# Batched 64x64 matrix multiply: two of the eight a tiles loaded by two casting transfers with 8 KB runs

## The chip, the cores and the metric

The kernel runs on one core of one Trainium2 chip. The core has a matrix engine (TensorE), three engines for elementwise work (VectorE, ScalarE, GpSimd), SyncE, which here only issues transfers, and sixteen DMA engines that move data between HBM and the on-chip memory SBUF. The metric is the device time of one execution in microseconds (us). Of the kernel before, three runs gave a median of 133.72 us (133.55 to 133.87).

## What is computed

```python
# a, b: (1024, 64, 64) float32
def reference(a, b):
    return np.matmul(a, b).astype(np.float32)
```

There are 1,024 independent products of 64x64 matrices. 16.8 MB of a and 16.8 MB of b are read, and 16.8 MB are written.

## The kernel before

**Tiles.** The batch is cut into sixteen steps t of 64 matrices (`n_t`), and into eight a tiles s of 128 matrices (`n_s`), so that a tile s serves the steps 2s and 2s + 1. A b tile and an output tile belong to one step, 1 MB each; an a tile is 2 MB in HBM.

**How a is loaded.** `a_v` (L41) cuts an a tile into four quarters h: quarter h holds every fourth matrix, and each of the 128 partitions gets sixteen rows of one matrix, which lie together in HBM: a run of 4 KB. `load_a` (L70) loads quarters 0 to 2 through GpSimd's queue and lets the DMA cast them to bf16 on the way (L74, `a_sb`); quarter 3 goes through SyncE's queue as fp32 (L78, `a_raw`) and is cast by an engine. `a_sb` and `a_raw` each have three buffers (`A_AHEAD`). Tile 0 is loaded apart, all in fp32 and through SyncE and ScalarE (`load_first_a`, L81 to L92).

**How b is loaded and the result stored.** `load_b` (L94) issues even b tiles on SyncE's queue and odd ones on ScalarE's, as fp32 in runs of 512 B; there are three buffers. `cast` (L169) casts a b tile to bf16, on VectorE but for the first and half of the last. Stores (`put`, L194) go through GpSimd's queue up to step 13, and through SyncE's and ScalarE's for steps 14 and 15.

**What is done with a.** The product needs a transposed, and two neighbouring bf16 values are moved as one fp32 element. For tiles 1, 2 and 3 (`ON_DVE`) VectorE transposes in blocks of 32x32: `transpose_dve` (L116) handles two quarters a call, one transpose of 128x512 elements (L128) for a quarter. For quarter 3, ScalarE first casts `a_raw` (L126). The other tiles are regrouped by VectorE (`regroup`, L100; L109 for the cast quarters, L112 for the fp32 one) and transposed by TensorE (`transpose`, L133). `spread` (L146) then copies the transposed a into a block-diagonal matrix, of which there are two (`bd_tiles`); for tiles 1 to 3 these are eight VectorE copies of 32x512 a step (L154), for the others four of 32x1024 (L164).

**What is multiplied.** `multiply` (L187) does four matrix products for each of sixteen groups of four matrices with the block-diagonal a as the weights (L218), and copies the results from PSUM to `o_sb`, mostly on ScalarE (L206).

**Order.** The order of every engine and every queue is that of the program (`tc.manual_schedule()`, L239). Before the loop, the loads of tile 0, of b tiles 0 to 2 and of a tiles 1 and 2 are issued. Step 0 first puts `spread(1)` and `cast(1)` on VectorE, loads b tile 3, multiplies, transposes a tile 1, and then issues the loads of a tiles 3 and 4; tile 4 takes over the buffers of tile 1. Step 1 puts `spread(2)`, `cast(2)` and the load of b tile 4 in front of its product, and both halves of the transposition of a tile 2 behind it; steps 2 and 3 do the halves of tile 3. A store is issued one step after its product.

Of the kernel before, what the change touches and what calls it, by code (L numbers as in the profile page):

```python
# [8 lines left out]
fp32 = mybir.dt.float32  # L9
bf16 = mybir.dt.bfloat16  # L10
# [3 lines left out]
def kernel(  # L14
# [14 lines left out]
    nc = tc.nc  # L29
# [7 lines left out]
    N_BD = 2  # L37
    HOLD = 2
    ON_DVE = (1, 2, 3)

    a_v = a.rearrange("(s g h) (mp v) k -> s h g mp (v k)", h=4, g=32, v=16)  # L41
    b_v = b.rearrange("(t g h) (kp u) n -> t (h kp) g (u n)", h=4, g=16, u=2)
    o_v = out.rearrange("(t gh x) (mo w) n -> t (x mo) gh (w n)", gh=8, x=8, w=4)

    consts = ctx.enter_context(tc.tile_pool(name="consts", bufs=1))
    a_pool = ctx.enter_context(tc.tile_pool(name="a_pool", bufs=A_AHEAD))
    b_pool = ctx.enter_context(tc.tile_pool(name="b_pool", bufs=B_AHEAD))
    work = ctx.enter_context(tc.tile_pool(name="work", bufs=2))
# [13 lines left out]
    a_tiles, b_tiles, abf_tiles, at_tiles, bbf_tiles = {}, {}, {}, {}, {}  # L62
# [5 lines left out]
        return nc.scalar if t == n_t - 1 and lo % 4 == 0 else nc.sync  # L68

    def load_a(s):  # L70

        a_sb = a_pool.tile([128, 3, 16, 64], bf16, name="a_sb")
        for h in range(3):
            nc.gpsimd.dma_start(  # L74
                out=a_sb[:, h, :, :].rearrange("p v k -> p (v k)"), in_=a_v[s, h], single_packet=True
            )
        a_raw = a_pool.tile([128, 16, 64], fp32, name="a_raw")
        nc.sync.dma_start(out=a_raw[:].rearrange("p v k -> p (v k)"), in_=a_v[s, 3])  # L78
        a_tiles[s] = a_sb, a_raw

    def load_first_a():  # L81

# [17 lines left out]
    def regroup(s):  # L100
        a_sb = a_tiles.pop(s)
        a_bf = work.tile([128, 16, 4, 64], bf16, name="a_bf")
        if s == 0:
            for h in range(4):
                copy = nc.scalar.copy if h % 2 else nc.vector.tensor_copy
                copy(a_bf[:, :, h, :], a_sb[h].rearrange("p (v k) -> p v k", v=16))  # L106
        else:
            cast_sb, raw = a_sb
            nc.vector.tensor_copy(  # L109
                a_bf[:, :, 0:3, :], cast_sb[:].rearrange("p h v k -> p v h k")  # L110
            )
            nc.vector.tensor_copy(a_bf[:, :, 3, :], raw[:])  # L112
        abf_tiles[s] = a_bf
        at_tiles[s] = work.tile([128, 32, 4, 4, 4], fp32, name="at_sb")

    def transpose_dve(s, half):  # L116
        cast_sb, raw = a_tiles[s]
        if half == 0:
            at_tiles[s] = work.tile([128, 4, 8, 4, 4, 4], fp32, name="at_sb")
        for h in (2 * half, 2 * half + 1):  # L120
            rows = cast_sb[:, h, :, :] if h < 3 else None
            if h == 3:
                rows = work.tile([128, 16, 4, 64], bf16, name="a_bf")[:, 0:4, :, :].rearrange(
                    "p x y k -> p (x y) k"
                )
                nc.scalar.copy(rows, raw[:])  # L126
            pairs = rows.rearrange("p v k -> p (v k)").bitcast(fp32)
            nc.vector.transpose(  # L128
                at_tiles[s][:, h].rearrange("p g w mp vo -> p w vo g mp"),
                pairs.rearrange("p (vo w kp) -> p w vo kp", vo=4, w=4),  # L130
            )

    def transpose(s, j):  # L133
        a_cols = abf_tiles[s][:].rearrange("p v h k -> p v (h k)").bitcast(fp32)
        for wl in range(2):
            at_ps = t_psum.tile([128, 4, 128], fp32, name="at_ps")
            for vo in range(4):
                nc.tensor.transpose(  # L138
                    at_ps[:, vo, :], a_cols[:, 4 * vo + 2 * j + wl, :], identity[:]
                )  # L140
            nc.scalar.copy(  # L141
                at_tiles[s][:, :, 2 * j + wl, :, :],
                at_ps[:].rearrange("p vo (g mp) -> p g mp vo", mp=4),
            )

    def spread(t):  # L146
        bd = bd_tiles[t % N_BD]
        at_sb = at_tiles[t // 2]
        for h in range(4):
            rows = slice(32 * h, 32 * h + 32)  # L150
            if t // 2 in ON_DVE:
                for i in range(2):
                    block = 32 * (2 * (t % 2) + i)
                    nc.vector.tensor_copy(  # L154
                        bd[rows, 8 * i : 8 * i + 8, :, h, :, :].rearrange(
                            "p g w mp vo -> p (g w) (mp vo)"
                        ),
                        at_sb[block : block + 32, h].rearrange(
                            "p g w mp vo -> p (g w) (mp vo)"
                        ),  # L160
                    )
            else:
                half = slice(16 * (t % 2), 16 * (t % 2) + 16)
                nc.vector.tensor_copy(  # L164
                    bd[rows, :, :, h, :, :].rearrange("p g w mp vo -> p (g w) (mp vo)"),
                    at_sb[rows, half].rearrange("p g w mp vo -> p (g w) (mp vo)"),
                )
# [19 lines left out]
    def multiply(t):  # L187
# [20 lines left out]
        for half in range(2):  # L208
# [19 lines left out]
            if not last:  # L228
                copies = [nc.scalar.copy] * 4
                if half and t % 2 and t > 2 * max(ON_DVE):  # L230
                    copies[2:] = [nc.vector.tensor_copy] * 2
# [7 lines left out]
    with tc.manual_schedule():  # L239
# [7 lines left out]
        make_identity(nc, identity)  # L247
        nc.gpsimd.memset(bd_tiles[1][:, 0:8], 0.0)
        load_a(1)
        load_b(2)  # L250
        nc.gpsimd.memset(bd_tiles[1][:, 8:16], 0.0)
        load_a(2)
        regroup(0)
        transpose(0, 0)
        transpose(0, 1)
        spread(0)
        cast(0)
        for t in range(n_t):
            s, half = t // 2, t % 2
            if t + 1 < n_t:  # L260
                spread(t + 1)
                cast(t + 1)
            if t + B_AHEAD < n_t:
                load_b(t + B_AHEAD)
            if half == 0 and 0 < s < n_s - 1 - A_AHEAD:
                load_a(s + 1 + A_AHEAD)
            if half == 0 and 0 < s < n_s - 1 and s + 1 not in ON_DVE:
                transpose(s + 1, 1)
            multiply(t)
            if t == 0:  # L270
                transpose_dve(1, 0)
                transpose_dve(1, 1)
                a_tiles.pop(1)
                load_a(A_AHEAD)
                load_a(A_AHEAD + 1)
            if t and s + 2 in ON_DVE and (half or s):
                for part in [0, 1] if t == 1 else [half]:
                    transpose_dve(s + 2, part)
                if half:
                    a_tiles.pop(s + 2)  # L280
            elif half == 0 and 0 < s and s + 2 < n_s:
                regroup(s + 2)
            elif half == 1 and s + 2 < n_s:
                transpose(s + 2, 0)
            if t >= HOLD - 1:
                store(t - HOLD + 1)
# [32 lines left out]
```

## Time and profile before

The profiled execution took 133.61 us, of which the span of the program's instructions is 131.8 us.

| What | Value |
|---|---|
| Time of the profiled execution | 133.61 us |
| Span | 131.8 us |
| VectorE busy | 101.8 us (77%) |
| ScalarE busy | 88.1 us (67%) |
| TensorE matmul busy | 59.6 us (45%) |
| GpSimd busy | 31.9 us (24%) |
| Read from HBM and written to it | 33.55 MB and 16.78 MB, 382 GB/s over the span |
| Casting transfers of a (L74) | 21 of 256 KB as landed, 15.9 us from issue to landing in the median |
| Plain transfers of a (L78) | 7 of 512 KB, 17.3 us |
| Stores on GpSimd's queue (L195) | 14 of 1,024 KB, 22.7 us |

In the rows of forty slices each digit is the busy share of one fortieth of the span (3.3 us) in tenths, 9 standing for 90% and more. In the rows of DMA queues, q0 is GpSimd's, q1 SyncE's and q10 ScalarE's; they give packets, megabytes as landed, and the time that the packets took as a share of sixteen engines' span. In the rows by stretch, each engine has its busy time and the number of its instructions, and at the end stand the granted clock of TensorE, the DMA share and GB/s. In a timeline a row gives start, duration, engine (with a q for its queue), line, operation, what is written from what, and how many were merged. In a row of waits stand who waited, for whom, the total in us, how often, and the longest. Beside these views the trace holds a record of every DMA packet, with its start, duration, queue and size as landed.

### The profile page before, as it was taken

Reading aid. Unit: us, or ns where it says so; the run is one execution under the profiler, and the core shown is the slowest. Engines: PE = TensorE matmul, PEld = TensorE weight load, DVE = VectorE, ACT = ScalarE, POOL = GpSimd, SP = SyncE. Lnnn points to the kernel's source line nnn. Section 1 sums busy time; section 2 is a strip of 40 time slices with the busy share of each in tenths; the row PEclk is TensorE's granted clock in tenths of the full one; section 3 lists DMA queues with packets and bytes.
Section 4 is the critical chain, followed back from the end, with each engine's and each line's share of the span. In section 5 each row is a group of like instructions: output and inputs, shape, how many; then the busy total and the mean of one; then the engine's idle time right before and its main releaser. Section 6 shows DMA issues by size and latency. Waiting matters only on the chain.

```text
span 131.8 us, 2750 instructions
## 1 busy us (share of the span) xinstructions
PE 59.6 (45%) x1104; PEld 56.7 (43%) x1104; DVE 101.8 (77%) x144; ACT 88.1 (67%) x158; POOL 31.9 (24%) x43
## 2 busy tenths in 40 slices
PE   0006405730550640908662883299369619465000
PEld 0006305730550630908552872298368618464000
DVE  5930399529999984999999998699999997898300
ACT  2125414999495096492999989469969996549920
POOL 8991000340054000618031204300420302040000
PEclk9999975798568555595999599558968975579855
DMA  3999999999999999999999999999999999999993
GB/s 68 372 334 313 306 313 280 280 311 321 327 299 400 362 306 297 393 393 400 321 285 357 403 395 362 308 299 385 395 391 393 390 390 397 399 395 406 390 383 136
DMA packets 19020, 44.99 MB, mean 341 GB/s; under 512 B 1088, under 2 KB 3136, under 8 KB 19008
## 3 DMA queue, kind: packets, MB, share of 16 engines
q0 software_dynamic: 6832, 20.19, 50.6%
q1 hardware_dynamic: 7120, 14.68, 30.7%
q10 hardware_dynamic: 5056, 9.96, 20.1%
q8 instruction: 8, 0.13, 0.4%
q14 instruction: 4, 0.03, 0.1%
HBM read 33.55 MB, written 16.78 MB: 382 GB/s over the span
## 4 chain that ended last, share of the span: by engine, by line
DMA 53%; ACT 15%; DVE 14%; PE 6%; issue 5%; SPq 2%; ACTq 0%; DVEq 0%
DMA b_sb<-in_b_dram 53%; ACT o_sb L206 12%; PE o_ps L218 6%; DVE at_bd L164 4%; DVE b_bf L173 4%; DVE at_bd L154 2%; ACT b_bf L173 1%; DVE at_sb L128 1%; DVE o_sb L206 1%; DVE a_bf L109 1%; SPq L91 1%; ACT a_bf L126 1%; SPq L97 1%; ACT b_bf L180 1%; DVE a_bf L112 0%
## 5 line engine op out<-in xcount | busy, mean ns | idle before, releaser
L206 ACT COPY o_sb<-o_ps 64x512 f32<-64x512 f32 x112 | 65.0, 581 | 17.9 <-PE o_ps L218 13.5
L218 PEld LDWEIGHTS <-at_bd 128*128 128x128 bf16 x1024 | 45.2, 117 | 52.6 <-DVE b_bf L173 40.5
L218 PE MATMUL o_ps<-b_bf,at_bd 128*128 128x64 bf16 x960 | 45.6, 223 | 48.7 <-DVE b_bf L173 35.0
L164 DVE COPY at_bd<-at_sb 32x1024 f32<-32x1024 f32 x40 | 29.6, 739 | 6.6 <-ACT at_sb L141 5.6
L195 POOL DMA_DIRECT2D out_dram<-o_sb x14 | 15.4, 1103 | 46.1 <-ACT at_sb L141 20.6
L154 DVE COPY at_bd<-at_sb 32x512 f32<-32x512 f32 x48 | 22.0, 457 | 1.1
L74 POOL DMA_DIRECT2D a_sb<-in_a_dram x21 | 12.4, 606 | 38.5 <-DVE at_sb L128 33.2
L173 DVE CAST b_bf<-b_sb 128x2048 bf16<-128x2048 f32 x14 | 17.2, 1227 | 5.2 <-DMA b_sb<-in_b_dram 4.9
L138 PE MATMUL at_ps<-identity,a_bf 128*128 128x128 f32 x80 | 12.9, 329 | 11.0 <-ACT a_bf L106 11.0
L138 PEld LDWEIGHTS at_ps<-identity,a_bf 128*128 128x128 f32 x80 | 11.7, 176 | 11.0 <-issue 11.0
L141 ACT COPY at_sb<-at_ps 128x512 f32<-128x512 f32 x20 | 10.8, 591 | 2.7 <-PE at_ps L138 2.0
L128 DVE STREAM_TRANSPOSE at_sb<-a_sb 128x512 f32<-128x512 f32 x9 | 8.9, 1065 | 0.0
L128 DVE STREAM_TRANSPOSE at_sb<-a_bf 128x512 f32<-128x512 f32 x3 | 3.1, 1049 | 4.0 <-ACT a_bf L126 4.0
L206 DVE COPY o_sb<-o_ps 64x512 f32<-64x512 f32 x8 | 5.5, 690 | 0.2
L106 ACT CAST a_bf<-o_sb 128x1024 bf16<-128x1024 f32 x2 | 2.1, 1045 | 5.0 <-DMA o_sb<-in_a_dram 5.0
L173 ACT CAST b_bf<-b_sb 128x2048 bf16<-128x2048 f32 x1 | 1.9, 1897 | 4.0 <-DMA b_sb<-in_b_dram 4.0
L126 ACT CAST a_bf<-a_raw 128x1024 bf16<-128x1024 f32 x3 | 3.1, 1046 | 1.7 <-DMA a_raw<-in_a_dram 1.7
L109 DVE COPY a_bf<-a_sb 128x3072 bf16<-128x3072 bf16 x4 | 4.2, 1045 | 0.0
L106 DVE CAST a_bf<-o_sb 128x1024 bf16<-128x1024 f32 x2 | 2.8, 1383 | 1.8 <-DMA o_sb<-in_a_dram 1.8
L246 DVE MEMSET at_bd<- 128x4096 f32 x1 | 3.5, 3472 | 0.8 <-issue 0.8
L206 DVE COPY o_sb<-at_ps 64x256 f32<-64x256 f32 x8 | 3.4, 422 | 0.5 <-PE at_ps L218 0.4
L180 ACT CAST b_bf<-b_sb 128x512 bf16<-128x512 f32 x2 | 1.1, 616 | 3.5 <-DMA b_sb<-in_b_dram 3.5
(16 smaller groups left out, 15.4 us busy)
## 6 DMA issues: line engine op xcount, KB each, us to landing
out_dram<-o_sb POOLq DMA_DIRECT2D x14, 1024.0 KB, 22.7
a_sb<-in_a_dram POOLq DMA_DIRECT2D x21, 256.0 KB, 15.9
a_raw<-in_a_dram SPq DMA_DIRECT2D x7, 512.0 KB, 17.3
o_sb<-in_a_dram SPq DMA_DIRECT2D x2, 512.0 KB, 5.9
o_sb<-in_a_dram ACTq DMA_DIRECT2D x2, 512.0 KB, 7.0
out_dram<-o_sb SPq DMA_DIRECT2D x2, 512.0 KB, 5.5
out_dram<-o_sb SPq DMA_DIRECT2D x2, 256.0 KB, 5.2
out_dram<-o_sb ACTq DMA_DIRECT2D x2, 256.0 KB, 4.7
```

What stands on the lines that cost most here:

```text
L74: nc.gpsimd.dma_start(out=a_sb[:, h, :, :].rearrange("p v k -> p (v k)"), in_=a_v[s, h], single_packet=True)
L106: copy(a_bf[:, :, h, :], a_sb[h].rearrange("p (v k) -> p v k", v=16))
L109: nc.vector.tensor_copy(a_bf[:, :, 0:3, :], cast_sb[:].rearrange("p h v k -> p v h k"))
L128: nc.vector.transpose(at_tiles[s][:, h].rearrange("p g w mp vo -> p w vo g mp"), pairs.rearrange("p (vo w kp) -> p w vo kp", vo=4, w=4),)
L138: nc.tensor.transpose(at_ps[:, vo, :], a_cols[:, 4 * vo + 2 * j + wl, :], identity[:])
L141: nc.scalar.copy(at_tiles[s][:, :, 2 * j + wl, :, :], at_ps[:].rearrange("p vo (g mp) -> p g mp vo", mp=4),)
L154: nc.vector.tensor_copy(bd[rows, 8 * i : 8 * i + 8, :, h, :, :].rearrange("p g w mp vo -> p (g w) (mp vo)"), at_sb[block : block + 32, h]. ...
L164: nc.vector.tensor_copy(bd[rows, :, :, h, :, :].rearrange("p g w mp vo -> p (g w) (mp vo)"), at_sb[rows, half].rearrange("p g w mp vo -> p ...
L173: (nc.vector.tensor_copy if t else nc.scalar.copy)(b_bf[:], b_sb[:])
L195: store_queue(t, lo).dma_start(out=o_v[t, :, lo : lo + n, :], in_=o_sb[:, lo : lo + n].rearrange("p gh j wl n -> p (gh j wl n)"),)
L206: copies[2 * par + wl](dst, src)
L218: nc.tensor.matmul(o_ps[:, gl, g % 2, j, :], at_bd[:, j, g, :, u], b_bf[:, g, 64 * u : 64 * u + 64], start=(u == 0), stop=(u == 1),)
```

## The change

The a tiles 2 and 3 (`LONG_RUNS`) are loaded by two casting transfers each instead of three casting ones and a plain one. The view `a_v8` gives a partition 32 rows of one matrix, a run of 8 KB, and a transfer holds every second matrix. Their transposition has one instruction of 128x1024 elements a half, without ScalarE's cast, and `spread` takes its blocks from the new layout. For every tile the cast part and the fp32 quarter now lie in one buffer (`room`) of the same total size.

```diff
+    LONG_RUNS = (2, 3)
+    a_v8 = a.rearrange("(s g h) (mp v) k -> s h g mp (v k)", h=2, g=64, v=32)
...
     def load_a(s):
-        a_sb = a_pool.tile([128, 3, 16, 64], bf16, name="a_sb")
+        room = a_pool.tile([128, 5120], bf16, name="a_sb")
+        if s in LONG_RUNS:
+            a_sb = room[:, 0:4096].rearrange("p (h x) -> p h x", h=2)
+            for h in range(2):
+                nc.gpsimd.dma_start(out=a_sb[:, h, :], in_=a_v8[s, h], single_packet=True)
+            a_tiles[s] = a_sb
+            return
+        a_sb = room[:, 0:3072].rearrange("p (h x) -> p h x", h=3)
         for h in range(3):
-            nc.gpsimd.dma_start(
-                out=a_sb[:, h, :, :].rearrange("p v k -> p (v k)"), in_=a_v[s, h], single_packet=True
-            )
-        a_raw = a_pool.tile([128, 16, 64], fp32, name="a_raw")
-        nc.sync.dma_start(out=a_raw[:].rearrange("p v k -> p (v k)"), in_=a_v[s, 3])
-        a_tiles[s] = a_sb, a_raw
+            nc.gpsimd.dma_start(out=a_sb[:, h, :], in_=a_v[s, h], single_packet=True)
+        raw = room[:, 3072:5120].bitcast(fp32)
+        nc.sync.dma_start(out=raw, in_=a_v[s, 3])
+        a_tiles[s] = (
+            a_sb.rearrange("p h (v k) -> p h v k", v=16),
+            raw.rearrange("p (v k) -> p v k", v=16),
+        )
...
     def transpose_dve(s, half):
+        if s in LONG_RUNS:
+            if half == 0:
+                at_tiles[s] = work.tile([128, 2, 8, 4, 4, 8], fp32, name="at_sb")
+            nc.vector.transpose(
+                at_tiles[s][:, half].rearrange("p g w gm vo -> p w vo g gm"),
+                a_tiles[s][:, half, :].bitcast(fp32).rearrange(
+                    "p (vo w kp) -> p w vo kp", vo=8, w=4
+                ),
+            )
+            return
...
     def spread(t):
...
                     block = 32 * (2 * (t % 2) + i)
+                    src = at_sb[block : block + 32]
+                    if t // 2 in LONG_RUNS:
+                        pair = 2 * (h // 2)
+                        src = src[:, h % 2, :, :, pair : pair + 2, :]
+                    else:
+                        src = src[:, h]
                     nc.vector.tensor_copy(
...
-                        at_sb[block : block + 32, h].rearrange(
-                            "p g w mp vo -> p (g w) (mp vo)"
-                        ),
+                        src.rearrange("p g w mp vo -> p (g w) (mp vo)"),
```

More of the change, by code (lines that the diff above doesn't have):

```diff
@@ L109, in regroup @@
             nc.vector.tensor_copy(
-                a_bf[:, :, 0:3, :], cast_sb[:].rearrange("p h v k -> p v h k")
+                a_bf[:, :, 0:3, :], cast_sb.rearrange("p h v k -> p v h k")
             )
-            nc.vector.tensor_copy(a_bf[:, :, 3, :], raw[:])
+            nc.vector.tensor_copy(a_bf[:, :, 3, :], raw)
         abf_tiles[s] = a_bf
@@ L125, in transpose_dve @@
                 )
-                nc.scalar.copy(rows, raw[:])
+                nc.scalar.copy(rows, raw)
             pairs = rows.rearrange("p v k -> p (v k)").bitcast(fp32)
```

## The prediction

> **What bounds the kernel now.** I read the slices first, then the queues, the stretches, the waits, and last the order of single instructions.
>
> ```profile
> DVE  5930399529999984999999998699999997898300
> ACT  2125414999495096492999989469969996549920
> DMA  3999999999999999999999999999999999999993
> DMA packets 19020, 44.99 MB, mean 341 GB/s; under 512 B 1088, under 2 KB 3136, under 8 KB 19008
> ...
> q0 software_dynamic: 6832, 20.19, 50.6%
> q1 hardware_dynamic: 7120, 14.68, 30.7%
> q10 hardware_dynamic: 5056, 9.96, 20.1%
> ```
>
> The DMA row has a 9 in every slice but the first and the last, and the queues' shares add up to 101.4% of sixteen engines' span. VectorE is the only other row that is near full, and only from slice 9 to slice 34.
>
> ```profile
> core 0: us, PE busy (x) PEld busy (x) DVE busy (x) ACT busy (x) POOL busy (x), PEclk, DMA share, GB/s
> ...
> 20.00:40.00 20.00, 9.35 (x192) 8.87 (x191) 15.75 (x24) 15.95 (x27) 4.87 (x8) 0.70 1.08 305
> ...
> 92.00:117.00 25.00, 15.47 (x301) 14.79 (x302) 23.09 (x30) 18.82 (x35) 5.85 (x5) 0.73 1.03 393
> 117.00:126.00 9.00, 2.38 (x72) 2.14 (x69) 5.39 (x12) 8.48 (x18) 0.07 (x1) 0.88 1.03 397
> 126.00:131.80 5.80, 0.00 (x0) 0.00 (x0) 0.00 (x0) 0.24 (x1) 0.00 (x0) 0.50 0.70 244
> ```
>
> The DMA share is 1.03 to 1.08 in every stretch up to 126 us, the last of them included, where only stores are left. The 305 GB/s of the early stretch is no slack: bytes are counted as they land, and a casting transfer lands half of what it reads. Counted as read, the packet records give 390 to 409 GB/s in every 3 us from 6 to 123 us. So the end is set by the sum of the DMA work, and a wait elsewhere costs time only if it empties the queues. By issues less packets moved, 4 to 7 MB (10 us of work or more) wait in the queues from 10 us to 110 us, 1.4 MB at 122 us. The chain of waits agrees: 53% of it is b tiles in flight.
>
> **The change, part by part.** Durations below are of the profiled execution (133.61 us, span 131.8, 1.8 us around it); the median of the runs is 133.72, and differences carry over to it.
>
> *Packets.* Sorted by queue and size, the packet records have: 4 KB read and cast to 2 KB, 172 ns, 2,688 times; plain packets of 1, 2 and 4 KB, 46, 84 and 159 ns at their undisturbed values, and of 8 KB (ten, loaded with the program) 310 ns at the fastest. Twice 46 less 84 is 8, twice 84 less 159 is 9, twice 159 less 310 is 8: each packet has some 9 ns that do not grow with its bytes. While casts run, packets overlap (share 1.08): from 12 to 15 us one cast and two 2 KB packets, 172 + 95 + 84 = 351 ns by their durations, moved 8 KB of source per engine at 403 GB/s, which is 8192 / 25.2 = 325 ns. So a 4 KB cast really takes 325 - 2 x 84 = 157 ns, as much as a plain one. Tiles 2 and 3 now have 2 x (3 x 128 casts + 128 plain) = 1,024 packets of 4 KB source; they become 2 x 2 x 128 = 512 of 8 KB. No 8 KB cast is in this trace. Lower bound of the saving: the run is moved as two 4 KB pieces, 0. Upper: all of 172 above the 2 x (159 - 84) = 150 ns of data is per packet, 22 ns, which gives 512 x 22 / 16 = 0.70 us. Below zero: 8 KB takes twice 172 with no overlap, 512 x (344 - 2 x 157) / 16 = 0.96 us lost. I take 9 ns, the plain rows' figure, since the cast's true 157 ns is nearest to theirs: 512 x 9 / 16 = 0.29 us saved.
>
> *The plain quarter.* 256 plain packets become cast bytes. Beside casts they took 170 to 172 ns, as a cast does, and 159 alone: 0, within 256 x 13 / 16 = 0.2 us either way.
>
> *Fewer transfers.* Eight transfers become four. Each ends in a 4-byte packet per engine of 9 ns: 4 x 9 = 0.04 us. Nothing else counts, since with queues that never empty one transfer's completion lies under the next one's packets. The Trainium skill's page "DMA: Bandwidth & Descriptors" (Anatomy of one DMA — SWDGE (gpsimd) path) gives each transfer a fixed cost of about 2.0 us besides its bytes; by it alone four fewer would be worth an estimated 8 us, and the DMA row without a gap says that this cost is hidden here.
>
> *Engines.* ScalarE loses two casts of L126 (1.05 us each), and VectorE no longer waits for them; both lie beside the DMA. Eight transposes of 128x512 (L128, 1,065 ns) become four of 128x1024: 8.5 us if time follows elements, 4.3 if it were fixed; I take 8.4. The 32 copies of L154 for tiles 2 and 3 read 16-element blocks that lie 32 apart, where they read on without gaps. They write such blocks already, so I keep 419 ns; the bound is the 690 ns of VectorE's copy of 512 elements at L206, 32 x 0.27 = 8.7 us.
>
> *GpSimd and SyncE queues.* Both parts of a tile now share one buffer. The casts of tile 4 took over only the cast part's buffer of tile 1 (three transposes, 25.2 us); now they wait for ScalarE's cast of tile 1 too, at 28.9. Behind them stands the first store (28.1, then some 30.6). Tile 4 landed at 42.3 and is first read at 59.6, so 17 us cover this. GpSimd's wait at 11.45 (1.67 us, for a free completion slot) goes. On SyncE the plain loads of tiles 2 and 3 go; that of tile 4 waits for the same ScalarE cast as before, with b tile 4 behind it.
>
> ```profile
> 10.05 0.71 SPq L97 DMA_DIRECT2D b_sb<-in_b_dram  x1
> 10.81 18.66 SPq L78 DMA_DIRECT2D a_raw<-in_a_dram  x3
> 29.93 0.82 SPq L97 DMA_DIRECT2D b_sb<-in_b_dram  x1
> ...
> 29.84 3.44 DVE L154 COPY at_bd<-at_sb 32x512 f32<-32x512 f32 x8
> 33.30 1.23 DVE L173 CAST b_bf<-b_sb 128x2048 bf16<-128x2048 f32 x1
> ...
> DVE b_bf L173 <- DMA b_sb<-in_b_dram: 4.9, 3, 2.0
> ```
>
> SyncE issues b tile 2, then three plain quarters back to back, then b tile 4; VectorE casts b tile 2 at 33.30 and waits for b tiles three times in all.
>
> *Whose packets go first.* This is the price of the change. From 12 to 15 us the three queues moved 46, 51 and 53 packets per us: one for one. A queue's share then follows its packet size. Before, of 8 KB per turn 4 KB were b; now, of 12 KB, again 4. Tiles 2 and 3 are 32 such turns of 310 + 2 x 84 = 478 ns, 15 us in which the b queues get 1 MB less. It is the megabyte of plain quarters that SyncE's queue no longer carries, but those stood behind b tile 2. So b tiles 2 and 3 bear it: half a megabyte at 0.1 MB per us (2 KB x 16 per 325 ns) is 5 us. Tile 2 landed at 32.0 and would land at about 37; its cast (33.30, right behind the copies of L154, so just in time) moves to 37.3, and everything on VectorE behind it by 4 us. I put 0 on it, for three reasons. The queues still hold about 2 MB: 6.3 at 42 us, less the plain quarter (0.5), the casts of tile 5 (1.6) and two stores (2.1) that would be issued after that. VectorE later sits idle for b tiles for 2.0 us (until 51.2), 1.6 (83.7) and 1.2 (112.5), 4.8 together (the last line above), and b tile 4 has no plain quarters ahead of it any more. And the last store piece is issued at 126.27 while packets run until 130.6, so some 2 us of lateness stay hidden even at the end. The Trainium skill's "DMA: Bandwidth & Descriptors" (SWDGE vs HWDGE vs iDMA) prefers packets of at most 4096 B, as a DMA engine changes queues only between packets; that rule speaks against 8 KB runs, and its price would be this same delay.
>
> Sum: -0.29 - 0.04 + 0 = -0.33; 133.61 becomes 133.28, the median 133.72 becomes **133.4**.
>
> **Rivals.**
> *The long run is cut* into two 4 KB packets: only 0.04 us is left, 133.7. For it: no dynamic packet here is over 4 KB. Against: plain 8 KB packets exist.
> *A cast of 8 KB stalls its engine* (two times 172, nothing overlapped): 0.96 - 0.04, 134.6. For it: 172 is above the plain 159, and the eight 16 KB packets that load code took 967 ns, over three times the 8 KB ones. Against: the throughput shows the excess hidden.
> *b tile 2 is late and stays late* (the slower side by order, not by work): place, the VectorE cast of b tile 2; it decides once more than 2 us are left at the last tile. If none of the 4 us is made up, 4 - 2 = 2 us, 135.4 with the saving. For it: VectorE is 92% busy from 92 to 117 us. Against: the three idle stretches.
> *The 22 ns are all saved*: 0.70 + 0.04, 133.0.
>
> **How the numbers follow.** Forecast 0.46, cut 0.18, stall 0.15, late 0.14, all saved 0.07. The forecast's own range is 133.2 to 133.6, the 0.2 us either way of the plain quarter. The range 132.9 to 134.7 takes in all but the late b tile, which leaves out some 0.17 in all. About 0.2% (0.27 us) is what a measurement of this kernel can tell from no change. Faster by that: 0.38 of the forecast's 0.46 and the 0.07, 0.45. Same: the rest of the forecast and the cut, 0.26. Slower: 0.29.
>
> **What would show it.** Right: queue 0's packets fall from 6,832 to 6,544 (768 casts become 512, and two transfers of 16 completions go; with the runs cut there are 1,024 casts and it rises to 7,056), 8 KB casts last 310 to 330 ns, DMA stays at 9 throughout, b tile 2 lands near 37 us and VectorE's lateness is gone by its wait near 83 us. Wrong: 8 KB casts of 344 ns, L154's copies of these tiles well over 419 ns, or a slice after 117 us below 9 in the DMA row. That would make the end a matter of order, and my sum of packets would not hold.

## The result and the profile after

The changed kernel took 134.48 us in the median of seven runs (134.06 to 134.92), the kernel before 133.72 us in seven runs on the same chip (133.46 to 133.94): the ratio is 1.0054 (interval 1.0035 to 1.0074). It is slower by 0.7 us, where a gain of 0.33 us was forecast: the interval lies clear of no change, on the other side. The profiled execution took 134.31 us, its span 132.5 us.

The slices, packets and queues of the kernel after:

```profile
DVE  5930197908599999999999999599999998696600
DMA  3999999999999999999999999999999999999993
GB/s 73 360 338 310 307 281 281 249 278 312 301 276 330 400 328 275 361 393 404 323 283 354 399 395 365 306 297 387 398 390 393 388 392 394 398 400 404 391 377 133
DMA packets 18444, 44.47 MB, mean 336 GB/s; under 512 B 1024, under 2 KB 3072, under 8 KB 18432
...
q0 software_dynamic: 6544, 20.71, 51.9%
q1 hardware_dynamic: 6832, 13.63, 28.8%
q10 hardware_dynamic: 5056, 9.96, 20.5%
```

By these lines the change did what it says: queue 0 has 6,544 packets, as worked out, and the DMA row still holds a 9 in every slice but the first and the last. Nothing in that row tells that this execution is slower. The next view is the waits of the kernel after (who waited, for whom, total in us, times, the longest), and after it the timelines of GpSimd, of ScalarE's cast of tile 1 and of VectorE's casts of b, each after and then before:

```profile
POOL a_sb L82 <- ACT a_bf L145: 21.3, 1, 21.3
...
POOL a_sb L82 <- DVE at_sb L129: 18.7, 2, 10.1
```

```profile
30.40 1.74 POOL L82 DMA_DIRECT2D a_sb<-in_a_dram  x3 [21.34 <-ACT a_bf L145]
32.11 0.94 POOL L218 DMA_DIRECT2D out_dram<-o_sb  x1
...
41.63 1.79 POOL L82 DMA_DIRECT2D a_sb<-in_a_dram  x3 [8.59 <-DVE at_sb L129]
```

```profile
25.23 1.61 POOL L74 DMA_DIRECT2D a_sb<-in_a_dram  x3 [13.25 <-DVE at_sb L128]
...
37.65 1.69 POOL L74 DMA_DIRECT2D a_sb<-in_a_dram  x3 [8.62 <-DVE at_sb L128]
```

```profile
29.06 1.05 ACT L145 CAST a_bf<-a_sb 128x1024 bf16<-128x1024 f32 x1
```

```profile
27.85 1.05 ACT L126 CAST a_bf<-a_raw 128x1024 bf16<-128x1024 f32 x1
```

```profile
36.45 1.23 DVE L196 CAST b_bf<-b_sb 128x2048 bf16<-128x2048 f32 x1 [1.40 <-DMA b_sb<-in_b_dram]
...
52.29 1.23 DVE L196 CAST b_bf<-b_sb 128x2048 bf16<-128x2048 f32 x1
...
84.52 1.23 DVE L196 CAST b_bf<-b_sb 128x2048 bf16<-128x2048 f32 x1 [1.56 <-DMA b_sb<-in_b_dram]
```

```profile
51.23 1.23 DVE L173 CAST b_bf<-b_sb 128x2048 bf16<-128x2048 f32 x1 [2.04 <-DMA b_sb<-in_b_dram]
...
83.66 1.23 DVE L173 CAST b_bf<-b_sb 128x2048 bf16<-128x2048 f32 x1 [1.63 <-DMA b_sb<-in_b_dram]
```

GpSimd stood for 21.3 us in front of the casts of tile 4, until ScalarE's cast of tile 1 had freed the shared buffer, and issued them at 30.40 us instead of 25.23. That cast itself came 1.2 us later than before: ahead of it on ScalarE stands the work on b tile 0, whose cast started at 20.45 us instead of 19.23. b tile 2 landed at 36.43 us and was cast at 36.45 (before: 33.30). The casts of b tiles 4 and 9 start at 52.29 and 84.52 (before: 51.23 and 83.66).

Where the time went is read from the packet records. In this table every packet counts with the bytes it reads (a cast twice what lands), b packets are those of both queues, and the casts are those that all sixteen engines moved in that us:

```
            before                        after
us          GB/s read  b packet           GB/s read  b packet   casts per us
30 to 31    396        92 ns              405        89 ns      29 (of 8 KB)
31 to 32    407        86 ns              378        91 ns      4
32 to 33    406        86 ns              302        115 ns     1
33 to 34    407        86 ns              290        118 ns     0
34 to 35    408        84 ns              292        118 ns     0
35 to 36    408        85 ns              392        98 ns      40
```

After is ahead of before by 0.35 us of bytes at 30 us (in units of 0.4 MB per us), even at 33, and behind by 0.60 us at 36. (Such figures hold the start of the execution too: at 10 us, before any 8 KB cast of tiles 2 and 3, this trace is 0.1 us behind before, and those of the kernels below that load tile 1 as before lie between level and 0.2 us ahead.) It stays 0.5 to 0.6 us behind until 129 us, and the span is 0.7 us longer. So the whole loss, some 0.95 us, falls between 31 and 36 us. There the casts of tile 3 had ended (all but a few by 31.6 us, the last at 32.5), queue 0 held nothing more until 35.1 us, and the b tiles alone did not keep the DMA engines at their rate: packets that took 84 to 92 ns took up to 118. A slow packet counts as busy as a fast one (the DMA share is 1.05 in this stretch), and so the row of tenths shows nothing.

### The profile page after: what moved, and what is told of

The parts are those of the page before. It is cut to its first block, busy times and chain, and to the rows that moved or that the text cites. A ratio compares the mean times of both kernels' runs of the same rounds, so it can differ in the third digit from the quotient of the medians.

```text
span 132.5 us, 2744 instructions
## 1 busy us (share of the span) xinstructions
PE 62.5 (47%) x1104; PEld 59.7 (45%) x1104; DVE 102.2 (77%) x140; ACT 86.0 (65%) x156; POOL 31.9 (24%) x41
## 3 DMA queue, kind: packets, MB, share of 16 engines
q0 software_dynamic: 6544, 20.71, 51.9%
## 4 chain that ended last, share of the span: by engine, by line
DMA 44%; DVE 29%; ACT 9%; SPq 7%; issue 5%; PE 1%; DVEq 0%; ACTq 0%
DMA b_sb<-in_b_dram 44%; ACT o_sb L229 8%; DVE at_bd L179 8%; DVE at_bd L187 6%; DVE b_bf L196 6%; DVE at_sb L129 6%; SPq L84 5%; DVE a_bf L118 2%; PE o_ps L241 1%; SPq L106 1%; DVE o_sb L229 1%; SPq L100 1%; DVE a_bf L121 1%; ACT b_bf L203 1%; ACT at_sb L160 0%
## 5 line engine op out<-in xcount | busy, mean ns | idle before, releaser
L241 PEld LDWEIGHTS <-at_bd 128*128 128x128 bf16 x1024 | 47.4, 120 | 51.7 <-DVE b_bf L196 40.1
L241 PE MATMUL o_ps<-b_bf,at_bd 128*128 128x64 bf16 x960 | 46.1, 224 | 47.9 <-DVE b_bf L196 38.4
L179 DVE COPY at_bd<-at_sb 32x512 f32<-32x512 f32 x48 | 22.5, 469 | 1.1
L82 POOL DMA_DIRECT2D a_sb<-in_a_dram x15 | 9.5, 643 | 43.9 <-ACT a_bf L145 21.3
L157 PE MATMUL at_ps<-identity,a_bf 128*128 128x128 f32 x80 | 13.8, 346 | 11.6 <-ACT a_bf L115 11.6
L157 PEld LDWEIGHTS at_ps<-identity,a_bf 128*128 128x128 f32 x80 | 12.7, 187 | 11.6 <-issue 11.6
L129 DVE STREAM_TRANSPOSE at_sb<-a_sb 128x1024 f32<-128x1024 f32 x4 | 7.7, 1956 | 0.0
L241 PE MATMUL at_ps<-b_bf,at_bd 128*128 128x64 bf16 x64 | 3.6, 242 | 1.2 <-DVE at_bd L187 1.2
L147 DVE STREAM_TRANSPOSE at_sb<-a_bf 128x512 f32<-128x512 f32 x1 | 1.1, 1077 | 3.7 <-ACT a_bf L145 3.7
## 6 DMA issues: line engine op xcount, KB each, us to landing
out_dram<-o_sb POOLq DMA_DIRECT2D x14, 1024.0 KB, 21.3
```

The costliest lines, as they stand in the source:

```text
L82: nc.gpsimd.dma_start(out=a_sb[:, h, :], in_=a_v[s, h], single_packet=True)
L129: nc.vector.transpose(at_tiles[s][:, half].rearrange("p g w gm vo -> p w vo g gm"), a_tiles[s][:, half, :].bitcast(fp32).rearrange("p (vo ...
L157: nc.tensor.transpose(at_ps[:, vo, :], a_cols[:, 4 * vo + 2 * j + wl, :], identity[:])
L179: nc.vector.tensor_copy(bd[rows, 8 * i : 8 * i + 8, :, h, :, :].rearrange("p g w mp vo -> p (g w) (mp vo)"), src.rearrange("p g w mp vo -> ...
L241: nc.tensor.matmul(o_ps[:, gl, g % 2, j, :], at_bd[:, j, g, :, u], b_bf[:, g, 64 * u : 64 * u + 64], start=(u == 0), stop=(u == 1),)
```

## The experiments

Two theories stood at the start. **D** (dry queue): GpSimd's DMA queue runs empty because the casts of tile 4 are issued too late, and b packets alone are slow. **L** (late b): b tile 2 comes late, VectorE stays late, and the end moves with it. Within D, either the runs of 512 B are what makes b slow when it is alone (D1), or two queues alone can't fill the engines (D2). "L82" and the like are the lines of each kernel itself. All were timed in five rounds against the kernel before on the same chip, whose median was 133.45 us for the own buffer of tile 4, the shared buffer alone, the earlier cast and the four casts, 133.48 us for b in 2 KB runs and for four buffers, and 133.54 us for the two buffers apart and the memsets. Each ratio is taken from all runs of both kernels, and differs from the quotient of the medians by up to 0.0008.

**Casts of tile 4 in a buffer of their own.**

```diff
-        a_sb = room[:, 0:3072].rearrange("p (h x) -> p h x", h=3)
+        part = consts.tile([128, 3072], bf16, name="a_own") if s == 4 else room
+        a_sb = part[:, 0:3072].rearrange("p (h x) -> p h x", h=3)
```

> The changed kernel, but the casts of a tile 4 land in a buffer of their own, so that they wait for no engine. Theory D (dry queue): in the changed kernel the 8 KB casts gain some 0.3 us as forecast, and all of the loss lies between 31 and 35 us, where GpSimd's queue holds no packet because the casts of tile 4 wait for ScalarE's cast of tile 1 (until 30.1 us); what is left, 512 B runs of b alone, moves at 290 GB/s in place of 400. Then this kernel has no stretch under 390 GB/s between 6 and 120 us and takes 133.72 - 0.3 = 133.4 us, ratio 0.9975 to the kernel before. Theory L (late b): the end is later because b tiles 2 and 3 land later and VectorE stays behind; b tile 2 still lands at 36 us or later here, so the ratio stays at 1.005 (134.4 us).

Measured: 1.0059 (1.0047 to 1.0072), 134.3 us: a miss for D as I had put it. The trace shows the stretch at 31 to 35 us gone, and after 42 us it is 0.5 us ahead of before. But a new stretch of the same kind lies at 43.5 to 46.5 us (296 to 319 GB/s, b packets of 108 to 117 ns). Its reason stands in GpSimd's timeline of this kernel:

```profile
42.08 1.79 POOL L83 DMA_DIRECT2D a_sb<-in_a_dram  x3 [12.01 <-DVE at_sb L130]
```

The casts of tile 5 wait for VectorE's transposes of tile 2, which stand behind the late b tile 2; before, they were issued at 37.65. The late b tile costs time after all, but through the same empty queue, once more. By the trace the last landing is then only 0.1 us later than in before; the rest of the longer span is the program's closing part, which grew by some 0.5 us (below).

**The two buffers apart again**, with the long runs kept: the reverse of the one moved wait.

```diff
-        room = a_pool.tile([128, 5120], bf16, name="a_sb")
+        room = a_pool.tile([128, 4096], bf16, name="a_sb")
+        quarter = a_pool.tile([128, 1024], fp32, name="a_raw")
...
-        raw = room[:, 3072:5120].bitcast(fp32)
+        raw = quarter[:]
```

> The change with the cast part and the fp32 quarter in buffers of their own again (three each, as before), so that the casts of tile 4 wait for three transposes of tile 1 alone. They are issued near 25 us, and the dry stretch at 31 to 35 us is gone. By the theory of the empty queue the second one, before the casts of tile 5 (issued near 42 us, since VectorE is late through b tile 2), stays as in e1 and costs 0.6 us against 0.3 gained: 1.002 to 1.004. If sharing the buffer were the whole cause, 0.997 to 0.999.

Measured: 1.0049 (1.0031 to 1.0067), 134.16 us, above what the theory gave; sharing as the whole cause falls. GpSimd's timeline of this kernel:

```profile
25.75 1.61 POOL L83 DMA_DIRECT2D a_sb<-in_a_dram  x3 [16.68 <-DVE at_sb L148]
29.51 0.92 POOL L219 DMA_DIRECT2D out_dram<-o_sb  x1 [2.15 <-ACT o_sb L230]
41.62 1.78 POOL L83 DMA_DIRECT2D a_sb<-in_a_dram  x3 [11.19 <-DVE at_sb L130]
```

From 31 to 35 us it moves 392 to 402 GB/s, and at 44 to 46 us 344 and 302. After the second stretch it is 0.1 us ahead of before, at 129 us 0.1 us behind; its last landing is 0.1 us later than in before, and the closing part 0.5 us longer. Undoing the shared buffer alone thus moves the dry stretch and does not win the gain; most of what this kernel's span is longer by lies in the closing part.

**The shared buffer alone**, without long runs.

```diff
-    LONG_RUNS = (2, 3)
+    LONG_RUNS = ()
```

> The changed kernel with no tile in 8 KB runs: of the change only the shared buffer is left, so all transfers are those of the kernel before, but the casts of tile 4 wait for ScalarE's cast of tile 1 (28.9 us) in place of the third transpose (25.2 us). D: first packets come some 4.4 us after the issue, as in the changed kernel, at 33.3 us, while tile 3's last casts are through at about 31.8; so the queue is dry for 1 to 1.5 us and 0.3 to 0.4 us are lost: 134.0 to 134.1 us, ratio 1.002 to 1.003. L: the packets of b go as before, so no change, 133.7 us.

Measured: 1.0042 (1.0025 to 1.006), 134.11 us, more than expected. The casts of tile 4 were issued at 29.72 us, and queue 0 was empty from 31.35 to 33.63. The trace shows only some 0.24 us of lag by 129 us, and the rest in the last landings and in closing, in an execution (134.76) that is the longest of its twelve. So the wait alone costs time, some 0.2 us between 32 and 36 us; how much of the rest is its doing stays open. That this hole of 2.3 us cost so little has a reason in the same window, here and in the kernel before (the last figures are clock, DMA share and GB/s as landed):

```profile
32.00:34.00 2.00, 0.00 (x0) 0.00 (x0) 1.91 (x5) 1.96 (x4) 0.35 (x1) 0.79 1.06 364
```

```profile
32.00:34.00 2.00, 0.00 (x0) 0.00 (x0) 1.91 (x4) 1.63 (x3) 0.00 (x0) 0.50 1.08 320
```

Here SyncE's queue moved the plain quarters in packets of 4 KB beside the b packets, which took 91 ns, and 364 GB/s landed. In the change those of tiles 2 and 3 are gone, only b is left in the hole, and 293 GB/s land (window below). The 320 GB/s of before are with casts, which land half of what they read.

**ScalarE's cast of tile 1 put ahead of the copies of product 0.**

```diff
+            if t == 0:
+                cast_quarter(1)
             multiply(t)
```

> The changed kernel, with ScalarE's cast of tile 1's plain quarter put ahead of the eight copies of step 0's result. The shared buffer of tile 1 is then free after the transposes, at about 26.5 us, and the casts of tile 4 are issued some 3.5 us earlier. D: their first packets come at about 31 us, when tile 3's end; no dry stretch, 133.4 to 133.5 us, ratio 0.998. L: b tile 2 is as late as in the changed kernel and the first copies of step 0 are 1 us later, so 134.4 us or more.

Measured: 1.0024 (1.0012 to 1.0035), 133.85 us. The casts of tile 4 were issued at 26.72 us, and 31 to 35 us ran at 393 to 409 GB/s: half of the loss is gone. The casts of tile 5 still came late (41.13), and 44 to 46 us ran at 347 and 336 GB/s: the trace, 0.5 us ahead of before at 42 us, is 0.3 ahead at 48. This execution (133.51) is among the shorter ones of its kernel, and what the median of 133.85 lost besides is not seen in it.

**Four casts of 4 KB for tiles 2 and 3**, in the shared buffer: no fp32 quarter, but no long run either.

```diff
-            a_sb = room[:, 0:4096].rearrange("p (h x) -> p h x", h=2)
-            for h in range(2):
-                nc.gpsimd.dma_start(out=a_sb[:, h, :], in_=a_v8[s, h], single_packet=True)
+            a_sb = room[:, 0:4096].rearrange("p (h x) -> p h x", h=4)
+            for h in range(4):
+                nc.gpsimd.dma_start(out=a_sb[:, h, :], in_=a_v[s, h], single_packet=True)
```

> The changed kernel with the a tiles 2 and 3 in four casting transfers of 4 KB runs, and the transposes and copies of the kernel before: the plain quarter is gone and the buffer is shared, but no run is 8 KB. D: GpSimd's queue has 88 packets per engine ahead of tile 4 in place of 72, at one for one with b, so it lasts until about 36 us, and tile 4's first packets are there by 34.5: no dry stretch, nothing gained per packet either, 133.7 us, ratio 0.999 to 1.001. A theory that the missing plain quarter is what costs, by b's order or by GpSimd's share, gives 134.3 us, ratio 1.004.

Measured: 1.0025 (1.0013 to 1.0036), 133.89 us, between the two expectations. There is no dry stretch, b tile 2 lands at 31.34 us, and the trace lies level with before until 126 us. With 4 KB packets b tile 2 does not come late, and without a hole the missing plain quarter costs nothing that the trace shows; what the 0.3 us are that this kernel still loses, these traces don't show.

**b tiles 2 and 3 in runs of 2 KB**, all else as in the change. This decides between D1 and D2.

```diff
-        queue.dma_start(out=b_sb[:], in_=b_v[t])
+        if t in (2, 3):
+            queue.dma_start(out=b_sb[:].rearrange("p (c g) n -> p c (g n)", c=4), in_=b_w[t])
+        else:
+            queue.dma_start(out=b_sb[:], in_=b_v[t])
```

> The changed kernel, but b tiles 2 and 3 are read in runs of 2 KB in place of 512 B (other elements of the same 1 MB, so that the products of steps 2 and 3 are not the reference's); nothing else is moved. Theory D1: GpSimd's queue still runs dry from about 31 to 35 us, and what makes that stretch slow is that only 512 B runs of b are left; with 2 KB runs their packets take 84 to 90 ns in place of 118, the stretch moves 390 GB/s or more, and the time falls by about 0.9 us from 134.5: 133.5 us, ratio 0.998 to 1.000 to the kernel before. Theory D2: the stretch is slow because two queues alone cannot keep the engines at their rate, whatever the runs: 290 GB/s as before, ratio 1.005.

Measured: 0.9979 (0.9966 to 0.9992), 133.28 us: a gain of 0.28 us. Windows of the kernel after and, in the next fence, of this one:

```profile
32.00:34.00 2.00, 0.00 (x0) 0.00 (x0) 1.96 (x4) 1.95 (x4) 1.04 (x2) 1.00 1.05 293
```

```profile
32.00:34.00 2.00, 0.00 (x0) 0.00 (x0) 1.96 (x4) 1.95 (x4) 1.00 (x2) 0.85 1.06 409
```

Both kernels have the same hole in queue 0: here GpSimd issued the casts of tile 4 at 30.39 us, and queue 0 was empty from 31.17 to 34.16. In both only b packets run, and the DMA share is the same. But packets that read 2 KB in one piece took 84 to 86 ns, and 293 GB/s became 409. That decides for D1: a dry queue costs time here because of how b is read when it is alone. Two things changed together, though: by the view `b_v` a packet of 2 KB gathers four pieces of 512 B that lie 64 KB apart in HBM (every fourth matrix of 16 KB), and here it is one piece. Whether the length of the pieces or the distance between them makes a packet slow was not parted, and a right product with longer runs of b was not tried.

**Four a buffers**, in the change and in the kernel before.

```diff
-    a_pool = ctx.enter_context(tc.tile_pool(name="a_pool", bufs=A_AHEAD))
+    a_pool = ctx.enter_context(tc.tile_pool(name="a_pool", bufs=A_AHEAD + 1))
```

> The changed kernel with four shared buffers in place of three, and nothing else: the casts of tile 4 wait for no engine and those of tile 5 only for tile 1. Theory D: both dry stretches are lost (that of 31 to 35 us, and the one that came at 43 to 47 us when only tile 4 was freed, because VectorE, late by b tile 2, gave up tile 2's buffer late); no stretch under 380 GB/s between 6 and 120 us, and the gain of the 8 KB casts is left, 0.3 us or a little less by a late last step: ratio 0.997 to 0.999 to the kernel before. Theory L: b tile 2 lands at 36 us or later as before and VectorE is as late, so the ratio stays at 1.004 to 1.006.

> The kernel before with four buffers for each of its two a tiles' parts. D: it has no dry stretch to lose, so nothing is gained: ratio 0.998 to 1.002. If a fourth buffer is worth something by itself (more transfers in the queues, b tile 4 not behind a waiting transfer), this run shows how much of the run with four shared buffers is due to that.

Measured: 1.001 (0.9996 to 1.0023), 133.7 us, for the change, and 0.9993 (0.998 to 1.0005) for the kernel before. GpSimd's timeline and VectorE's casts of b in the change with four buffers:

```profile
14.25 0.53 POOL L82 DMA_DIRECT2D a_sb<-in_a_dram  x1 [2.25 <-DMA a_sb<-in_a_dram]
29.20 0.91 POOL L218 DMA_DIRECT2D out_dram<-o_sb  x1 [14.43 <-ACT o_sb L229]
30.27 1.71 POOL L82 DMA_DIRECT2D a_sb<-in_a_dram  x3 [0.16 <-issue]
```

```profile
37.08 1.23 DVE L196 CAST b_bf<-b_sb 128x2048 bf16<-128x2048 f32 x1 [2.65 <-DMA b_sb<-in_b_dram]
...
76.25 1.23 DVE L196 CAST b_bf<-b_sb 128x2048 bf16<-128x2048 f32 x1
83.79 1.23 DVE L196 CAST b_bf<-b_sb 128x2048 bf16<-128x2048 f32 x1 [1.77 <-DMA b_sb<-in_b_dram]
```

The last of the casts of tile 4 is now issued at 14.25 us, and those of tile 5 at 30.27. No stretch falls under 391 GB/s from 31 to 36 us, and the trace stays 0.5 us ahead of before from there to 123 us. Here b tile 2 is as late as in the change (cast at 37.08), and VectorE is level with before again at b tile 8 (76.25 in both). So L falls: a late b tile costs nothing while the casts' queue holds work. The last landing is at 130.46 us, 0.45 us earlier than before, and yet the span is 131.9 us.

**Tile 1 in long runs too**, with four buffers.

```diff
-    LONG_RUNS = (2, 3)
+    LONG_RUNS = (1, 2, 3)
```

> The changed kernel with four shared buffers and tile 1 in 8 KB runs as well. D: half as much again is saved per packet (768 merged packets, 0.43 us, and two more completions), and no queue runs dry: ratio 0.996 to 0.998. L: b tile 0 has the long packets beside it from the start, lands some 2.5 us later than in the kernel before, and every step is later than in the changed kernel: ratio 1.008 or more.

Measured: 1.0003 (0.9991 to 1.0016), 133.61 us. Again 0.6 to 0.7 us ahead of before until 126 us and the last landing early (130.25), and again a span of 131.7 us.

**The closing part.** From the last landing to the span's end the traces have 0.9 to 1.1 us in most kernels, but 1.4 to 1.5 us in four: the two with four buffers, and the two with apart buffers of tile 4 (in the kernel with the shared buffer alone it is 1.3 us, without the pause that follows). In these four GpSimd pauses for 0.4 us among the semaphore instructions of the end (130.78 to 131.20 us in the change with four buffers), and in these four alone the last 8 KB packet of program code begins at the span's end or after it, at 132.0 to 132.4 us instead of 123 to 130. The pages of the two with four buffers then count one packet fewer, since the last lies outside the span:

```profile
q14 instruction: 3, 0.02, 0.0%
```

To see whether it hangs on the place of GpSimd's instructions in memory, sixteen more were put into step 8, where GpSimd is idle (they took 4.7 us there):

```diff
+            if t == 8:
+                for _ in range(16):
+                    nc.gpsimd.memset(pad[:], 0.0)
```

> Four a buffers (e7) and sixteen GpSimd memsets of one column in step 8, where GpSimd has nothing to do; they only move GpSimd's later instructions by sixteen places. If the 0.42 us that GpSimd lost in the closing sequence of e7 hang on where its program code is cut into blocks, the stall goes: the span ends 0.9 to 1.0 us after the last landing and the ratio is 0.997 to 0.999. If the stall comes from the order of the completions or from the fourth buffer itself, it stays: 1.001 as in e7, and 1.4 us from landing to end.

> The same sixteen memsets in e10 (four buffers, tiles 1, 2 and 3 in long runs). By the block theory the stall goes and the ratio is 0.996 to 0.998, the fastest so far; else 1.000 as in e10.

> The kernel before with the same sixteen memsets. Before has no stall in its closing sequence. 0.9990 to 1.0010 if the memsets do nothing else; a stall that appears here (1.002 to 1.004) would also speak for the block theory, since only the place of the instructions has changed.

```
                                ratio to before (interval)   last landing  span   between
four buffers                    1.001  (0.9996 to 1.0023)    130.46        131.9  1.5
the same, 16 memsets            0.9982 (0.9968 to 0.9996)    130.22        131.3  1.0
four buffers, tiles 1 to 3      1.0003 (0.9991 to 1.0016)    130.25        131.7  1.5
the same, 16 memsets            0.9976 (0.9964 to 0.9989)    130.44        131.5  1.1
before, 16 memsets              1.0004 (0.999 to 1.0018)     130.57        131.5  0.9
```

The memsets do nothing for the kernel before and take 0.3 to 0.4 us off the two others. With them the closing part has its usual length, the last packets of code come at 128.1 and 129.0 us, and the page of the first counts four packets again:

```profile
q14 instruction: 4, 0.03, 0.1%
```

Nor do they hold up what follows: with four buffers the next store is issued at 79.52 us in place of 79.44, since GpSimd waited there without them. And the trace of the kernels with the pause holds 72 to 74 instructions of GpSimd, that of all others 75 to 92. That the pause hangs on where GpSimd's instructions lie is thereby shown. That it is a wait for program code is an inference: the late packet's record begins after the pause has ended. The kernel with four buffers, tiles 1 to 3 in long runs and the memsets has the lowest ratio, below 1 by more than its interval and well below the changed one; from the 0.9982 with tile 1 as before it does not part.

## Why the prediction was wrong

*The packets: right.* The casts of 8 KB are single packets of 322 ns (310 to 330 were given), two 4 KB ones at 172 ns are 344, and the rival that cuts the run falls. From 10 to 30 us the seven traces with tiles 2 and 3 alone in long runs gain 0.43 to 0.44 us on before, the four without long runs -0.02 to 0.04; with four buffers 0.35 of it is left at 36 us. In time 0.28 us remain with b in 2 KB runs and 0.24 us with four buffers and memsets, against 0.33 forecast. With tile 1 in long runs as well it is 0.32 us, where half as much again was expected: the range given for it, 0.996 to 0.998, just holds 0.9976. The 2.0 us that the Trainium skill's page "DMA: Bandwidth & Descriptors" (Anatomy of one DMA — SWDGE (gpsimd) path) gives a transfer do not appear in the time: with four transfers fewer and full queues the gain stays near 0.3 us.

*The engines: right.* The four transposes took 1,956 ns each, 7.8 us against 8.4. The copies for tiles 2 and 3 have a median of 419 ns in both traces.

*"GpSimd and SyncE queues": this step failed.* It priced the moved wait by when tile 4 is read: "Tile 4 landed at 42.3 and is first read at 59.6, so 17 us cover this." That a tile comes in time for its reader is one condition; the other is that the queue behind it never runs empty. The trace of before had the numbers. The last casts of tile 3 landed at 33.29 us. And GpSimd's first transfer, issued at 3.00 us, had its first packet at 7.14: 4.1 us. Moved from 25.23 to the forecast 28.9, the next packets would be due at 33.0, with 0.3 us of cover at most, and not 17. At most, since 33.29 is the landing on the last of the sixteen DMA engines: the fifteen others had moved these casts by 30.5 to 31.5 us, and would have had 1.5 to 2.5 us without them. The wait in fact ended at 30.40, because ScalarE's work on b tile 0 began 1.2 us later (20.45 instead of 19.23 us; the lateness was put on b tiles 2 and 3 alone), and nearly all the larger packets had ended by 31.6 us, so queue 0 stood empty until 35.1. The empty queue was named as a condition ("a wait elsewhere costs time only if it empties the queues") but checked on the sum of all three queues, 4 to 7 MB, and not on each.

*"The plain quarter": 0 as packets, but not for the order.* Its 4 KB packets were what SyncE's queue had beside b. With them a hole of 2.3 us cost some 0.2 us (the shared buffer alone, 364 GB/s landing); without them the hole of the change cost 0.95 us (293 GB/s), and with b in 2 KB runs nothing.

*"Whose packets go first": right in its size, wrong in its reasons for 0.* b tile 2 landed at 36.43 us, as forecast (37), and the lateness did shrink, though 0.9 us of it are left at 84 us. But the 2 MB that "the queues still hold" were counted over all queues: when queue 0 ran dry a second time, the others held b, which alone doesn't fill the engines. And what is late on VectorE is also late in giving back the buffers that the casts of tile 5 wait for. The kernels with tile 4's buffers apart show it: 0.4 to 0.6 us lost at 43 to 47 us. In the change itself queue 0 had the first store to move until 47 us, since everything in it ran later, and no second hole opened. One cause, an empty queue 0, thus stood in the way in two places: in the change at 31 to 35 us, and in these kernels at 43 to 47.

*"DMA stays at 9 throughout"* was given as a sign that the sum of packets holds. It came true and did not tell. The busy share counts a packet of 118 ns as full, as it does one of 84. What would have told is the time of one packet by its kind and the bytes read per us. (With each packet shared out over the stretches that it overlaps, those of 3 us before read at 388 to 415 GB/s, a little wider than the 390 to 409 given.)

*The rivals.* Cut, stall of 8 KB casts and late b all named other mechanisms; none had the empty queue. The measured 134.48 lies inside the 132.9 to 134.7 and near the 134.6 of the stalled casts, but by chance: that rival's own sign, casts of 344 ns, did not come. The empty queue's price by the rows of the trace: from 31 to 36 us, (405 - 378) + (405 - 302) + (405 - 290) + (405 - 292) + (405 - 392) KB, 371 KB or 0.92 us at 405 GB/s, less the 0.35 gained by 30 us: 0.57, close to the 0.60 that the trace is behind at 36 us. The last landing is 0.58 us later than in before, and the closing part takes 0.12 us more.

## What to carry to other kernels

Before two buffers are merged, look at when the queue of the waiting issue runs empty, counted from the first packet of the next transfer (here 4 us after its issue) and not at when the tile is read; the sixteen engines run empty at different times, so take the first and not the landing. Do this for each queue by itself, and ask what the remaining queues can move alone: here pieces of 512 B, 64 KB apart, gave 290 of 400 GB/s when nothing else was read. A DMA row full of nines shows busy engines, not full speed; compare the time of one packet of a kind along the span.

## What the runs showed of the hardware

A casting transfer into an empty queue had its first packet 3.8 to 4.7 us after the start of its issue (3.00 to 7.14 in before, 30.40 to 35.1 in after, 29.72 to 33.63 with the shared buffer alone, 30.39 to 34.16 with b in 2 KB runs). The Trainium skill's "DMA: Bandwidth & Descriptors" (Specifications, the table at its head) gives about 1 us to the first byte on this path; here the measurement decides.

b packets that gather runs of 512 B took 84 to 96 ns beside casts or stores, and 115 to 118 ns with only the other b queue beside them; those with runs of 2 KB took 84 to 86 ns alone. The same page's table (Specifications) takes 512 B as the size from which a transfer runs at line rate. Here pieces of 512 B that lay 64 KB apart gave 290 GB/s alone and about 400 beside other transfers, so the size by itself did not decide.

Sixteen more instructions on an idle engine (4.7 us together) shortened two kernels by 0.3 to 0.4 us, by way of the pause in the closing part, and left a third, which has no pause, as it was. A difference of that size between two kernels can thus come from where the instructions lie, and not from what they do.
